# Last output product of a two-layer block: residual, statistics and norm kept in the product's PSUM banks, and the high parts of its rows rounded by ScalarE

## The chip, the cores and the metric

The kernel runs on one core of one Trainium2 chip. The metric is the device time of one execution in microseconds; the median of three runs is used. A core has five engines that run side by side, each with its own queue of instructions taken in order: TensorE (PE in the rows; PEld is its load of stationary weights), VectorE (DVE), ScalarE (ACT), GpSimd (POOL) and SyncE (SP), which here only issues transfers. A trailing q (SPq, ACTq) marks the engine's sequencer, which issues transfers and waits on semaphores. SBUF is the on-chip working memory of 128 partitions, PSUM the memory into which TensorE writes its products: eight banks, each 128 partitions by 512 fp32 values. GpSimd has no access to PSUM in this kernel.

## The reference

Two layers over 1024 latent rows of width 1024 and a context of 256 rows. The first layer (pooling mixer and spatial gating) matters here only as the place of the first output product and its norm. The second layer mixes the rows by a Fourier mixer and by attention with eight heads, gates both, and ends with the step that the change is about:

```python
y = concatenate([yc, yd], axis=-1) @ w_out            # (1024 x 1024) @ (1024 x 1024)
r = ALPHA * x + gate * y                              # x: output of the first layer, gate: one row
mu, var = mean(r), mean((r - mu) ** 2)                # over the 1024 columns of a row
out = (r - mu) * rsqrt(var + EPS) * g + b
```

## The kernel before

Every matmul operand is fp32, cut into a high part (rounded to the fp32r type that TensorE takes) and a low part (the value less its high part); a product is three matmuls, high by high, high by low and low by high. `split` (L102 to L107) makes the two parts: a cast to the high part on VectorE ("v") or ScalarE ("s"), and a subtraction for the low part on VectorE or GpSimd ("p").

**The last product** works on eight row tiles t of 128 rows. `z_split` (L1330) makes yz, the stationary operand of a tile: it cuts the tile's columns of fg (Fourier half) and dg (attention half) into high and low parts, each 128x512; both casts run on VectorE, the low part of fg on VectorE, that of dg on GpSimd. Tiles 0 and 1 are cut near the end of the attention (`block_end`), tile t+2 in the round of tile t; there are two buffers. The weights of the product are four blocks z0 to z3 (wH_z, wL_z and wz in the rows), two for each half of the output columns, loaded through three shared raw buffers; z2 and z3 are cut after the attention, z2 by ScalarE and VectorE, z3 by ScalarE and GpSimd (L143 issues the loads).

The output of a tile is two halves of 512 columns, each summed in one PSUM bank over 24 matmuls (`y_mm`, at L442, of 48 per tile). The first halves of tiles 0 and 1 are made in the last part of the attention; from then on TensorE goes through tile 0 second half, tile 1 second half, tile 2, and so on. Tile 7 is done in four quarters of 256 columns. In this stretch the products take their banks from the four of tag mm; three more of tag tr are free. `z_row` (L1433 to L1437) loads a row tile of the first layer's normalised rows and applies that layer's g and b on GpSimd, two instructions of 128x1024; two buffers xf, tile t+2 again in the round of tile t.

For each half, `z_residual` does three VectorE passes: L1445 multiplies the bank by the gate into r in SBUF, L1446 adds ALPHA times xf, L1447 takes the statistics. Then per tile: L1466 joins the statistics, `rsqrt` (L216) takes a square root on ScalarE and does one Newton step in four instructions of 128x1 on VectorE (L227 to L230), L1477 subtracts the mean and multiplies by g, and L1481 multiplies by the reciprocal root and adds b. L1482 sends the first half from the SyncE queue, the second from ScalarE's. In tile 7, the second half's mean and g are done by ScalarE (L1474) and GpSimd (L1475) instead.

`rsqrt` with n of 1 is also used for the ten tiles of the first layer's norm. The attention's instructions are in an order written out by hand (letters that call pieces, and `pin` that keeps the program's order); the instructions of the last product's norm are not pinned: the framework orders each engine's queue when it builds the program, by the program's order and its own estimates, and puts in the semaphores.

Of the kernel before, what the change touches and what calls it, by code (L numbers as in the profile page):

```python
# [11 lines left out]
AF = mybir.ActivationFunctionType  # L12
ALU = mybir.AluOpType
# [4 lines left out]
P = 128  # L18
D = 1024
# [7 lines left out]
ALPHA = 4 ** 0.25  # L27
# [12 lines left out]
def _f(ap):  # L40
    return ap.bitcast(F32)


def hybrid_block(tc, A):
    nc = tc.nc
    ctx = ExitStack()
    with ctx:
        _body(nc, tc, A, ctx)


def _body(nc, tc, A, ctx):
    def pool(name, bufs=1, side=None, space=None, stack=ctx):
        kw = {}
        if side:
            kw["side"] = side
        if space is not None:
            kw["space"] = space
        return stack.enter_context(tc.tile_pool(name=name, bufs=bufs, reuse_waits="tile", **kw))
# [21 lines left out]
    def ps_mm(name, shape=(P, 512)):  # L80
        return psums[-1].tile(list(shape), F32, tag="mm", name=name, bufs=MM[len(psums)])
# [5 lines left out]
    keep = pool("keep")  # L87
# [15 lines left out]
    def split(dH, dL, src, h="v", l="p", ordered=False):  # L103

        keep = pin if ordered else (lambda ins: ins)
        keep(nc.vector.tensor_copy(dH, src) if h == "v" else nc.scalar.copy(dH, src))  # L106
        keep((nc.gpsimd if l == "p" else nc.vector).tensor_sub(dL, src, _f(dH)))  # L107
# [108 lines left out]
    def rsqrt(sp, v, n, name, bias=EPS, keep=lambda ins: ins):  # L216

        s = sp.tile([P, n], F32, tag="rs_s", name="rs_s" + name, bufs=2)
        e = sp.tile([P, n], F32, tag="rs_e", name="rs_e" + name, bufs=2)
        r = sp.tile([P, n], F32, tag="rs_r", name="rs_r" + name, bufs=2)  # L220
        t = sp.tile([P, n], F32, tag="rs_t", name="rs_t" + name, bufs=2)
        keep(nc.vector.tensor_scalar(e, v, 1.0, bias, op0=ALU.mult, op1=ALU.add))
        nc.scalar.activation(s, e, AF.Sqrt)
        keep(nc.vector.reciprocal(r, s))
        if n == 1:
            u = sp.tile([P, 2], F32, tag="rs_u", name="rs_u" + name, bufs=2)
            keep(nc.vector.scalar_tensor_tensor(t, r, e, r, op0=ALU.mult, op1=ALU.mult))  # L227
            keep(nc.vector.tensor_scalar(u[:, 0:1], r, -0.5, None, op0=ALU.mult))
            keep(nc.vector.tensor_scalar(u[:, 1:2], r, 1.5, None, op0=ALU.mult))
            keep(nc.vector.scalar_tensor_tensor(r, t, u[:, 0:1], u[:, 1:2], op0=ALU.mult, op1=ALU.add))  # L230
            return r
        keep(nc.vector.tensor_mul(t, r, r))
        keep(nc.vector.tensor_mul(t, t, e))
        keep(nc.vector.tensor_scalar(t, t, -0.5, 1.5, op0=ALU.mult, op1=ALU.add))
        keep(nc.vector.tensor_mul(r, r, t))
        return r
# [431 lines left out]
    def v_norm(t, vr):  # L668

        mv = sv.tile([P, 4, 2], F32, tag="mv", name="mv", bufs=2)  # L670
        for j in range(4):
            bs = sv.tile([P, 6], F32, tag="bs", name="bs", bufs=4)
            pin(nc.vector.bn_stats(bs, vr[:, j * P:(j + 1) * P]))
            pin(nc.vector.bn_aggr(mv[:, j, :], bs))
        rs = rsqrt(sv, mv[:, :, 1], 4, "v", keep=pin)
        vH = sv.tile([P, 512], F32R, tag="vH", name="vH", bufs=3)
        vL = sv.tile([P, 512], F32R, tag="vL", name="vL", bufs=3)
        for j in range(4):
            c = slice(j * P, (j + 1) * P)
            pin(nc.vector.tensor_scalar(vr[:, c], vr[:, c], mv[:, j, 0:1], rs[:, j:j + 1],  # L680
                                     op0=ALU.subtract, op1=ALU.mult))
        split(vH, vL, vr, "s", "v", True)
        for i in range(2):
            defer(10.5 + 2.6 * i, lambda i=i: v_gate(i, t, vH[:, i * 256:(i + 1) * 256], vL[:, i * 256:(i + 1) * 256]))
# [83 lines left out]
    def y_mm(ps, yhl, n, c=slice(0, 512)):  # L768

        half_mm(ps, lambda a, k: yhl[:, a, k, :], [x[:, :, c] for x in wo[n]], n % 2)  # L770
# [7 lines left out]
    def row_norm(sp, r, bs, name):  # L778
        mv = sp.tile([P, 2], F32, tag="mv", name="mv" + name, bufs=2)
        nc.vector.bn_aggr(mv, bs.rearrange("p a b -> p (a b)"))  # L780
        rs = rsqrt(sp, mv[:, 1:2], 1, name)
        nb = sp.tile([P, 1], F32, tag="nb", name="nb" + name, bufs=2)
        nc.vector.tensor_scalar(nb, mv[:, 0:1], rs, -1.0, op0=ALU.mult, op1=ALU.mult)
        return rs, nb
# [22 lines left out]
    for t in range(NT):  # L807
        src = A["x"][t * P:(t + 1) * P, :] if t < NL else A["ctx"][(t - NL) * P:(t - NL + 1) * P, :]
# [10 lines left out]
        xt = wp.tile([P, D], F32, tag="raw", name=f"xr{t}", bufs=3)  # L819
        nc.sync.dma_start(out=xt, in_=src)  # L820
        r = S567[t // 4][:, (t % 4) * D:(t % 4 + 1) * D]
        bs = lp.tile([P, 2, 6], F32, tag="bs", name=f"bs{t}", bufs=2)
# [55 lines left out]
    for t in range(NT):  # L878
        lat = t < NL
        c0 = 0 if lat else 256  # L880
        ps = ps_mm("ps_c")
# [147 lines left out]
    mid, rows, yb = {}, {}, None  # L1029
# [114 lines left out]
    for ot, q in units[3:]:  # L1144
        ps = ps_mm("ps_y")
# [184 lines left out]
    def z_split(t, sp):  # L1330
        s = slice(t * P, (t + 1) * P)
        yhl = sp.tile([P, 2, KT, P], F32R, tag="yhl", name=f"yz{t}", bufs=2)
        for i, src in enumerate((fg, dg)):
            k = slice(4 * i, 4 * i + 4)
            split(yhl[:, 0, k], yhl[:, 1, k], src[:, :, s], "v", "p" if i else "v")
        return yhl

    NB = HEADS * 4
# [4 lines left out]
    def block_end(B):  # L1343

        if B == NB - 3:
            st_k.close()
            tail["stack"] = ExitStack()
            fin0 = pool("fin0", stack=tail["stack"])
            tail["y"] = [z_split(t, fin0) for t in range(2)]
        clock[0] += 8.0  # L1350
        tick()
# [74 lines left out]
    gate1 = fin.tile([P, D], F32, name="gate1")  # L1426
    nc.sync.dma_start(out=gate1, in_=gate1_d.partition_broadcast(P))
    vec = {}
# [4 lines left out]
    def z_row(t):  # L1433
        xt = fin.tile([P, D], F32, tag="xt", name=f"xf{t}", bufs=2)
        nc.sync.dma_start(out=xt, in_=xn_d[t * P:(t + 1) * P, :])
        nc.gpsimd.tensor_mul(xt, xt, vec["ab_ln_g"])
        nc.gpsimd.tensor_add(xt, xt, vec["ab_ln_b"])  # L1437
        return xt
# [2 lines left out]
        wo.append(W.use(f"z{n}", ahead=False))  # L1441
    xr = {0: z_row(0), 1: z_row(1)}

    def z_residual(r, bs, ps, c, xt, i):
        nc.vector.tensor_mul(r[:, c], ps, gate1[:, c])  # L1445
        nc.vector.scalar_tensor_tensor(r[:, c], xt[:, c], ALPHA, r[:, c], op0=ALU.mult, op1=ALU.add)  # L1446
        nc.vector.bn_stats(bs[:, i, :], r[:, c])  # L1447

    for t in range(NL):
        last = t == NL - 1  # L1450
        parts = 4 if last else 2
        wd = D // parts
        r = fin.tile([P, D], F32, tag="r", name=f"rz{t}", bufs=2)
        bs = fin.tile([P, 4, 6], F32, tag="bs", name=f"bz{t}", bufs=2)
        for q in range(parts):
            ps = ps_of.get((t, q))
            if ps is None:
                ps = ps_mm("ps_z")
                for n in range(2):
                    y_mm(ps[:, :wd], yz[t], 2 * (q * wd // 512) + n, slice(q * wd % 512, q * wd % 512 + wd))  # L1460
            z_residual(r, bs, ps[:, :wd], slice(q * wd, (q + 1) * wd), xr[t], q)
        if t + 2 < NL:
            yz[t + 2] = z_split(t + 2, fin)
            xr[t + 2] = z_row(t + 2)
        mv = fin.tile([P, 2], F32, tag="mvz", name="mvz", bufs=2)
        nc.vector.bn_aggr(mv, bs[:, :parts].rearrange("p a b -> p (a b)"))  # L1466
        if last:
            nm = fin.tile([P, 1], F32, name="nm")
            nc.vector.tensor_scalar(nm, mv[:, 0:1], -1.0, None, op0=ALU.mult)
        rs = rsqrt(fin, mv[:, 1:2], 1, f"z{t}")  # L1470
        for q in range(2):
            c = slice(q * 512, (q + 1) * 512)
            if last and q:
                nc.scalar.activation(r[:, c], r[:, c], AF.Identity, bias=nm, scale=1.0)  # L1474
                nc.gpsimd.tensor_mul(r[:, c], r[:, c], vec["cd_ln_g"][:, c])  # L1475
            else:
                nc.vector.scalar_tensor_tensor(r[:, c], r[:, c], mv[:, 0:1], vec["cd_ln_g"][:, c],  # L1477
                                               op0=ALU.subtract, op1=ALU.mult)
        for q in range(2):
            c = slice(q * 512, (q + 1) * 512)  # L1480
            nc.vector.scalar_tensor_tensor(r[:, c], r[:, c], rs, vec["cd_ln_b"][:, c], op0=ALU.mult, op1=ALU.add)  # L1481
            (nc.scalar if q else nc.sync).dma_start(out=A["out"][t * P:(t + 1) * P, c], in_=r[:, c])  # L1482
    st_f.close()
    st_ps[0].close()

# [81 lines left out]
```

## Time and profile before

| what | value |
|---|---|
| median of three runs | 1137.46 us (1137.27 to 1138.54) |
| the profiled execution | 1138.53 us |
| its span, first to last instruction | 1136.7 us |
| TensorE busy, mean granted clock | 1077.7 us (95%), 0.977 of full speed |
| VectorE busy | 827.1 us (73%) |
| ScalarE busy | 456.3 us (40%) |
| GpSimd busy | 524.2 us (46%) |

Times in a profile are microseconds from the start of the span. A timeline row gives start, duration, engine, line, operation, output and inputs with their shape, a count of merged instructions, and in brackets how long the engine stood idle before it and what ended that. A duration can hold the time in which an instruction stands in its engine before it can go on. The busy share of a whole kernel is a mean over stages with different limits; the last 100 us are one such stage.

### The profile page before, as it was taken

How to read it: one execution, taken by the hardware profiler on the slowest of the kernel's cores; microseconds unless marked ns; L12 is line 12 of the kernel's file. 1: busy time of each engine (PE TensorE's matmuls, PEld its weight loads, DVE VectorE, ACT ScalarE, POOL GpSimd, SP SyncE). 2: the span in 40 equal slices, each digit the busy share in tenths (PEclk: the TensorE clock that was granted, in tenths of full speed). 3: DMA queues.
4: the chain of work that ended last, by engine and by line, in shares of the span. 5: the costliest groups of instructions: out<-in, count | busy, mean ns of one | idle time of the engine just before them, and what ended most of it. 6: DMA issues, size and time to landing. Idle time of an engine off the chain costs nothing.

```text
span 1136.7 us, 16517 instructions
## 1 busy us (share of the span) xinstructions
PE 1077.7 (95%) x5986; PEld 917.5 (81%) x5986; DVE 827.1 (73%) x1713; ACT 456.3 (40%) x1096; POOL 524.2 (46%) x449
## 2 busy tenths in 40 slices
PE   6999999899999999999999999999999999999884
PEld 4788887778878888897888877889899898887664
DVE  4683547899987767767200175988999989977998
ACT  3421222221211233531021244887888888860000
POOL 2362321555563433112481234855556556657442
PEclk7999999989999999999999999999999999999897
DMA  9630110235543322404311110000000010214221
GB/s 345 222 95 29 47 56 1 60 108 168 166 156 122 104 101 71 148 1 154 106 56 37 34 53 22 1 1 2 1 1 1 1 57 1 75 38 143 85 77 67
DMA packets 46993, 85.58 MB, mean 75 GB/s; under 512 B 2928, under 2 KB 27632, under 8 KB 46912
## 3 DMA queue, kind: packets, MB, share of 16 engines
q1 hardware_dynamic: 44096, 76.60, 21.2%
q0 software_dynamic: 1664, 5.84, 1.4%
q10 hardware_dynamic: 1152, 2.10, 0.5%
q8 instruction: 47, 0.77, 0.3%
q14 instruction: 34, 0.28, 0.1%
HBM read 76.13 MB, written 8.39 MB: 74 GB/s over the span
## 4 chain that ended last, share of the span: by engine, by line
PE 65%; DVE 23%; issue 4%; POOL 3%; ACT 3%; DMA 1%; SPq 0%; DVEq 0%; POOLq 0%; ACTq 0%
PE ps_mm L210 19%; PE ps_o L442 10%; PE s L1096 8%; PE ps_n L442 6%; PE av L1314 5%; PE pt_p L1289 5%; PE acc L363 2%; PE ps_y L1049 2%; DVE acc L499 2%; DVE mx L1255 2%; DVE rz L1477 2%; PE ps_c L210 2%; DVE rz L1446 1%; PE pq L1106 1%; DVE rs_tz L227 1%
## 5 line engine op out<-in xcount | busy, mean ns | idle before, releaser
L1096 PE MATMUL s<-kT,qT 96*128 96x512 f32 (+1 forms) x576 | 147.8, 370 | 3.7 <-ACT p L1267 2.7
L1267 ACT ACTIVATE p<-s,mx 128x512 f32<-128x512 f32 (+1 forms) x192 | 118.7, 624 | 17.1 <-DVE mx L1278 16.1
L1255 DVE TENSOR_REDUCE mx<-s 128x1 f32<-128x512 f32 (+1 forms) x192 | 112.1, 594 | 8.9 <-PE s L1096 7.0
L1298 DVE TENSOR_TENSOR pT<-pt_p,pT 128x512 fp32r<-128x512 f32 x160 | 108.1, 684 | 10.1 <-ACT pT L1294 8.1
L1275 POOL TENSOR_SCALAR p<-p,mx 128x1280 f32<-128x1280 f32 x64 | 85.6, 1341 | 42.1 <-ACT pT L1294 11.9
L1096 PEld LDWEIGHTS s<-kT,qT 96*128 96x128 f32 x576 | 90.7, 189 | 16.3 <-ACT p L1267 6.3
L1294 ACT CAST pT<-pt_p 128x512 fp32r<-128x512 f32 x160 | 92.8, 587 | 19.6 <-PE pt_p L1289 12.3
L1289 PE MATMUL pt_p<-ident,p 128*128 128x128 f32 x640 | 92.9, 273 | 0.9 <-DVE kT L1202 0.5
L1314 PE MATMUL av<-pT,V 128*128 128x256 f32 x480 | 78.9, 291 | 2.1 <-DVE pT L1298 2.1
L1289 PEld LDWEIGHTS pt_p<-ident,p 128*128 128x128 f32 x640 | 74.4, 140 | 7.4 <-ACT q L1112 1.1
L1314 PEld LDWEIGHTS av<-pT,V 128*128 128x128 f32 x480 | 67.5, 189 | 6.8 <-DVE pT L1298 2.5
L442 PE MATMUL ps_o<-wo,yhl 128*128 128x512 f32 x240 | 57.2, 391 | 0.0
L442 PE MATMUL ps_o<-wH_o,yhl 128*128 128x512 f32 x160 | 53.8, 397 | 0.0
L210 PE MATMUL ps_mm<-h,wH_u 128*128 128x512 f32 (+1 forms) x192 | 53.4, 367 | 0.0
L442 PE MATMUL ps_n<-wH_v,h 128*128 128x512 f32 x160 | 52.1, 395 | 0.0
L442 PEld LDWEIGHTS ps_o<-wo,yhl 128*128 128x128 f32 x240 | 44.8, 188 | 9.1
L442 PE MATMUL ps_z<-wz,yz 128*128 128x512 f32 (+1 forms) x216 | 47.3, 376 | 4.8 <-POOL wz L107 2.4
L210 PE MATMUL ps_mm<-h,wH_gb 128*128 128x512 f32 (+1 forms) x192 | 51.7, 357 | 0.0
L210 PE MATMUL ps_mm<-h,wH_ga 128*128 128x512 f32 (+1 forms) x192 | 51.2, 354 | 0.0
L442 PEld LDWEIGHTS ps_z<-wz,yz 128*128 128x128 f32 x216 | 38.2, 193 | 13.0 <-POOL wz L107 2.9
L442 PE MATMUL ps_z<-wH_z,yz 128*128 128x512 f32 (+1 forms) x112 | 36.8, 408 | 8.2 <-DVE yz L106 7.4
L210 PE MATMUL ps_c<-wH_c,h 128*128 128x416 f32 (+1 forms) x160 | 42.3, 341 | 0.0
(390 smaller groups left out, 2876.2 us busy)
## 6 DMA issues: line engine op xcount, KB each, us to landing
rawmm<-in_cd_w_mod SPq DMA_DIRECT2D x16, 512.0 KB, 3.6
wm<-in_ab_w_mod SPq DMA_DIRECT2D x6, 1024.0 KB, 8.2
S<-in_xT SPq DMA_DIRECT2D x8, 640.0 KB, 7.6
rawmg<-in_ab_w_mod SPq DMA_DIRECT2D x8, 512.0 KB, 3.6
raw_o<-in_ab_w_out SPq DMA_DIRECT2D x8, 512.0 KB, 3.8
xr<-in_x SPq DMA_DIRECT2D x8, 512.0 KB, 3.5
xn_d<-S POOLq DMA_DIRECT2D x8, 512.0 KB, 3.0
rawmg<-in_cd_w_mod SPq DMA_DIRECT2D x8, 512.0 KB, 4.3
```

Source lines behind the costliest of these rows:

```text
L210: nc.tensor.matmul(out, lhsT=a, rhs=b, start=(i == 0), stop=(i == n - 1))
L363: pin(nc.tensor.matmul(o, lhsT=a1[w][:, k, c], rhs=tok(h0, K0, x, k, a0, nt), start=(k + n == 0 and j == js[0]), stop=(k == KT - 1 and n = ...
L442: nc.tensor.matmul(ps, lhsT=lhsT(a, kk), rhs=w[b][:, k, :], start=(kk + i == 0), stop=(kk == KT - 1 and i == 2))
L499: pin(nc.vector.scalar_tensor_tensor(o, raw[:, c], s, o, op0=ALU.mult, op1=ALU.add))
L1096: pin(nc.tensor.matmul(out, lhsT=a, rhs=b, start=(i == 0), stop=(i == 2)))
L1255: pin(nc.vector.tensor_reduce(out=mx[:, j:j + 1], in_=ps, axis=AX.X, op=ALU.max))
L1267: pin(nc.scalar.activation(p32[:, e0:e0 + en], sc[e], AF.Exp, bias=mx[:, 3:4], scale=1.0, accum_out=mx[:, 4 + e:5 + e]))
L1275: pin(nc.gpsimd.tensor_scalar(p32, p32, mx[:, 8:9], 1.0, op0=ALU.mult, op1=ALU.mult))
L1289: pin(nc.tensor.transpose(pt[:, kk * 256 + i * P:kk * 256 + (i + 1) * P], P_of[2 * B + i][:, k * P:(k + 1) * P], ident))
L1294: pin(nc.scalar.copy(pT_of[B, kp][:, 0, :], pt))
L1298: pin(nc.vector.tensor_sub(pT[:, 1, :], pt, _f(pT[:, 0, :])))
L1314: pin(nc.tensor.matmul(av, lhsT=vv, rhs=pT[:, hl, kk * 256:(kk + 1) * 256], start=(k == 0 and hl == 0), stop=(k == NT - 1 and hl == 1)))
```

## The change

In the last product, `z_residual` works in place in the product's bank: gate, residual and statistics read the bank, and the first two write it. L1477 works in place in the bank too, and L1481 reads the bank and writes r in SBUF, from where it is sent. Odd parts of a tile take their bank from tag tr, even ones from tag mm. In tile 7 the mean, g and b are applied in quarters (two by VectorE, two by ScalarE and GpSimd, of which ScalarE reads the bank and writes r); its two transfers stay halves. `z_split` makes all casts on ScalarE and all subtractions on GpSimd. In `rsqrt` with n of 1, two instructions on 128x1 change from scalar_tensor_tensor (two tensors and a scalar) to tensor_scalar (one tensor and two scalars per partition).

```diff
--- before.py
+++ after.py
@@ -224,10 +224,10 @@
         keep(nc.vector.reciprocal(r, s))
         if n == 1:
             u = sp.tile([P, 2], F32, tag="rs_u", name="rs_u" + name, bufs=2)
-            keep(nc.vector.scalar_tensor_tensor(t, r, e, r, op0=ALU.mult, op1=ALU.mult))
+            keep(nc.vector.tensor_scalar(t, r, e, r, op0=ALU.mult, op1=ALU.mult))
             keep(nc.vector.tensor_scalar(u[:, 0:1], r, -0.5, None, op0=ALU.mult))
             keep(nc.vector.tensor_scalar(u[:, 1:2], r, 1.5, None, op0=ALU.mult))
-            keep(nc.vector.scalar_tensor_tensor(r, t, u[:, 0:1], u[:, 1:2], op0=ALU.mult, op1=ALU.add))
+            keep(nc.vector.tensor_scalar(r, t, u[:, 0:1], u[:, 1:2], op0=ALU.mult, op1=ALU.add))
             return r
         keep(nc.vector.tensor_mul(t, r, r))
         keep(nc.vector.tensor_mul(t, t, e))
@@ -1332,7 +1332,7 @@
         yhl = sp.tile([P, 2, KT, P], F32R, tag="yhl", name=f"yz{t}", bufs=2)
         for i, src in enumerate((fg, dg)):
             k = slice(4 * i, 4 * i + 4)
-            split(yhl[:, 0, k], yhl[:, 1, k], src[:, :, s], "v", "p" if i else "v")
+            split(yhl[:, 0, k], yhl[:, 1, k], src[:, :, s], "s", "p")
         return yhl
 
     NB = HEADS * 4
@@ -1441,10 +1441,11 @@
         wo.append(W.use(f"z{n}", ahead=False))
     xr = {0: z_row(0), 1: z_row(1)}
 
-    def z_residual(r, bs, ps, c, xt, i):
-        nc.vector.tensor_mul(r[:, c], ps, gate1[:, c])
-        nc.vector.scalar_tensor_tensor(r[:, c], xt[:, c], ALPHA, r[:, c], op0=ALU.mult, op1=ALU.add)
-        nc.vector.bn_stats(bs[:, i, :], r[:, c])
+    def z_residual(bs, ps, c, xt, i):
+
+        nc.vector.tensor_mul(ps, ps, gate1[:, c])
+        nc.vector.scalar_tensor_tensor(ps, xt[:, c], ALPHA, ps, op0=ALU.mult, op1=ALU.add)
+        nc.vector.bn_stats(bs[:, i, :], ps)
 
     for t in range(NL):
         last = t == NL - 1
@@ -1452,13 +1453,15 @@
         wd = D // parts
         r = fin.tile([P, D], F32, tag="r", name=f"rz{t}", bufs=2)
         bs = fin.tile([P, 4, 6], F32, tag="bs", name=f"bz{t}", bufs=2)
+        pss = []
         for q in range(parts):
             ps = ps_of.get((t, q))
             if ps is None:
-                ps = ps_mm("ps_z")
+                ps = (ps_tr if q % 2 else ps_mm)("ps_z")
                 for n in range(2):
                     y_mm(ps[:, :wd], yz[t], 2 * (q * wd // 512) + n, slice(q * wd % 512, q * wd % 512 + wd))
-            z_residual(r, bs, ps[:, :wd], slice(q * wd, (q + 1) * wd), xr[t], q)
+            pss.append(ps[:, :wd])
+            z_residual(bs, pss[q], slice(q * wd, (q + 1) * wd), xr[t], q)
         if t + 2 < NL:
             yz[t + 2] = z_split(t + 2, fin)
             xr[t + 2] = z_row(t + 2)
@@ -1468,18 +1471,22 @@
             nm = fin.tile([P, 1], F32, name="nm")
             nc.vector.tensor_scalar(nm, mv[:, 0:1], -1.0, None, op0=ALU.mult)
         rs = rsqrt(fin, mv[:, 1:2], 1, f"z{t}")
-        for q in range(2):
-            c = slice(q * 512, (q + 1) * 512)
-            if last and q:
-                nc.scalar.activation(r[:, c], r[:, c], AF.Identity, bias=nm, scale=1.0)
+        rows = []
+        for q, ps in enumerate(pss):
+            c = slice(q * wd, (q + 1) * wd)
+            if last and q > 1:
+                nc.scalar.activation(r[:, c], ps, AF.Identity, bias=nm, scale=1.0)
                 nc.gpsimd.tensor_mul(r[:, c], r[:, c], vec["cd_ln_g"][:, c])
+                rows.append(r[:, c])
             else:
-                nc.vector.scalar_tensor_tensor(r[:, c], r[:, c], mv[:, 0:1], vec["cd_ln_g"][:, c],
-                                               op0=ALU.subtract, op1=ALU.mult)
-        for q in range(2):
-            c = slice(q * 512, (q + 1) * 512)
-            nc.vector.scalar_tensor_tensor(r[:, c], r[:, c], rs, vec["cd_ln_b"][:, c], op0=ALU.mult, op1=ALU.add)
-            (nc.scalar if q else nc.sync).dma_start(out=A["out"][t * P:(t + 1) * P, c], in_=r[:, c])
+                nc.vector.scalar_tensor_tensor(ps, ps, mv[:, 0:1], vec["cd_ln_g"][:, c], op0=ALU.subtract, op1=ALU.mult)
+                rows.append(ps)
+        for q, row in enumerate(rows):
+            c = slice(q * wd, (q + 1) * wd)
+            nc.vector.scalar_tensor_tensor(r[:, c], row, rs, vec["cd_ln_b"][:, c], op0=ALU.mult, op1=ALU.add)
+            if parts == 2 or q % 2:
+                c = slice(q * 512 // (parts // 2) - (256 if parts == 4 else 0), (q + 1) * wd)
+                (nc.scalar if c.stop == D else nc.sync).dma_start(out=A["out"][t * P:(t + 1) * P, c], in_=r[:, c])
     st_f.close()
     st_ps[0].close()
 
```

## Rows read from the trace of the kernel before

**Rows 1.** The page's chain that ended last, shares of the span by engine.
```profile
PE 65%; DVE 23%; issue 4%; POOL 3%; ACT 3%; DMA 1%; SPq 0%; DVEq 0%; POOLq 0%; ACTq 0%
```
**Rows 2.** Stretch table: us, busy of PE, PEld, DVE, ACT, POOL, clock, DMA, GB/s.
```profile
360.00:475.00 115.00, 115.00 (x553) 96.83 (x552) 80.95 (x177) 38.13 (x66) 37.31 (x25) 1.00 0.32 104
...
980.00:1000.00 20.00, 20.00 (x143) 18.40 (x142) 18.33 (x46) 17.65 (x48) 11.65 (x11) 1.00 0.18 54
...
1039.00:1061.00 22.00, 22.00 (x98) 17.87 (x96) 21.89 (x31) 0.41 (x2) 13.36 (x6) 1.00 0.21 72
1061.00:1072.00 11.00, 6.79 (x17) 4.95 (x17) 10.97 (x16) 0.20 (x1) 6.08 (x3) 0.69 0.27 96
...
1091.60:1105.70 14.10, 11.54 (x48) 8.86 (x48) 13.85 (x21) 0.20 (x1) 6.49 (x3) 1.00 0.21 74
1105.70:1123.40 17.70, 14.92 (x96) 14.22 (x96) 17.31 (x31) 0.41 (x2) 6.41 (x3) 0.81 0.17 60
```
**Rows 3.** Timeline: VectorE and GpSimd side by side, 1031 to 1034 and 1093 to 1101.
```profile
1031.87 2.37 POOL L1436 TENSOR_TENSOR xf<-xf,v_ab_ln_g 128x1024 f32<-128x1024 f32 x1 [1.05 <-DMA xf<-xn_d]
...
1033.40 0.69 DVE L1445 TENSOR_TENSOR rz<-ps_z,gate 128x512 f32<-128x512 f32 x1 [5.45 <-PE ps_z L442]
...
1093.84 1.31 POOL L107 TENSOR_TENSOR yz<-dg,yz 128x512 fp32r<-128x512 f32 x1 [6.80 <-DVE mvz L1466]
1093.85 0.15 DVE L222 TENSOR_SCALAR rs_ez<-mvz 128x1 f32<-128x1 f32 x1
...
1095.51 2.45 POOL L1436 TENSOR_TENSOR xf<-xf,v_ab_ln_g 128x1024 f32<-128x1024 f32 x1 [0.37 <-DMA xf<-xn_d]
...
1095.69 2.82 DVE L1477 SCALAR_TENSOR_TENSOR rz<-rz,mvz,v_cd_ln_g 128x512 f32<-128x512 f32 x1
...
1098.04 2.73 POOL L1437 TENSOR_TENSOR xf<-xf,v_ab_ln_b 128x1024 f32<-128x1024 f32 x1
1098.43 2.36 DVE L227 SCALAR_TENSOR_TENSOR rs_tz<-rs_rz,rs_ez 128x1 f32<-128x1 f32 x1
```
**Rows 4.** Groups by form, busy us and mean ns; a transfer: KB, us to landing.
```profile
L1477 DVE SCALAR_TENSOR_TENSOR rz<-rz,mvz,v_cd_ln_g 128x512 f32<-128x512 f32 x15 | 23.1, 1554 | 0.0
...
L1445 DVE TENSOR_TENSOR rz<-ps_z,gate 128x512 f32<-128x512 f32 x14 | 9.4, 678 | 5.5 <-PE ps_z L442 5.4
...
L775 DVE SCALAR_TENSOR_TENSOR S<-xr,S 128x512 f32<-128x512 f32 x20 | 13.8, 689 | 0.3
...
L106 ACT CAST wH_z<-raw_z 128x512 fp32r<-128x512 f32 x8 | 5.0, 628 | 0.0
...
xf<-xn_d SPq DMA_DIRECT2D x8, 512.0 KB, 3.4
```
**Rows 5.** Timeline: TensorE where it had waited, tiles 4 and 7.
```profile
1065.42 0.80 PE L442 MATMUL ps_z<-wH_z,yz 128*128 128x512 f32 x1 [4.21 <-DVE yz L106]
...
1117.46 5.92 PE L442 MATMUL ps_z<-wz,yz 128*128 128x256 f32 x48 [2.33 <-DVE rz L1445]
```
**Rows 6.** Timeline: start of the stretch, last two weight blocks and second halves.
```profile
1017.40 2.95 ACT L106 CAST wz<-raw_z 128x1024 fp32r<-128x1024 f32 x3
...
1019.70 5.66 DVE L107 TENSOR_TENSOR wz<-raw_z,wz 128x1024 fp32r<-128x1024 f32 x2
...
1022.06 0.38 SPq L143 DMA_DIRECT2D raw_z<-in_cd_w_out  x1
...
1023.59 4.85 PE L442 MATMUL ps_z<-wz,yz 128*128 128x512 f32 x19
...
1028.48 2.34 POOL L107 TENSOR_TENSOR wz<-raw_z,wz 128x1024 fp32r<-128x1024 f32 x1
...
1030.87 8.36 PE L442 MATMUL ps_z<-wz,yz 128*128 128x512 f32 x29 [2.43 <-POOL wz L107]
```
**Rows 7.** Timeline: VectorE behind the last matmul.
```profile
1127.99 0.41 DVE L1445 TENSOR_TENSOR rz<-ps_z,gate 128x256 f32<-128x256 f32 x1
...
1130.88 1.03 DVE L227 SCALAR_TENSOR_TENSOR rs_tz<-rs_rz,rs_ez 128x1 f32<-128x1 f32 x1
```

## Prediction

> **What bounds the kernel now.** I read the chain that ended last first: TensorE holds 65% of it and VectorE 23% [rows 1]. Then the stretch table, to see where VectorE takes over. Through the first output product (360 to 475 us) TensorE is busy 115.00 of 115.00 us, and 20.00 of 20.00 near the end of the attention; from 1039 to 1061 it still runs without a gap, 22.00 us for two row tiles, so **11.0 us per tile** of 48 matmuls [rows 2]. [...] The timeline says why VectorE is slow. L1477 starts at 1095.69 and takes 2.82 us, ending as GpSimd's L1436 ends (1097.96); L227, on 128x1, starts at 1098.43 and takes 2.36 us, ending when GpSimd's L1437 ends (1100.77) [rows 3]. The same kinds of instruction take 0.69 us at 128x512 in the first layer [rows 4]. So a VectorE instruction that reads two tensors from SBUF stands still while GpSimd's two-tensor instruction runs. One that reads a product in PSUM and one SBUF tensor does not: L1445 at 1033.40 takes 0.69 us in the middle of GpSimd's L1436; nor does a one-tensor instruction on 128x1: L222 at 1093.85 takes 0.15 us beside GpSimd's 1.31 us subtraction [rows 3].
>
> **The change, term by term.**
>
> Waits removed. L1446 and L1477 get the product's bank as one operand, L227 and L230 become one-tensor instructions; L1481 of tiles 0 to 6 reads the bank too. The mean of L1477 is 1554 ns where the free price is 689 [rows 4]; in the round shown, its two runs and L227 alone stood about (1.69-0.65)+(2.82-0.65)+(2.36-0.15), some 5.4 us. The 1.69 and 0.65 are pitches of the chain; the two rows shown carry 2.2 each [rows 3].
>
> Casts moved. Per tile two casts (0.33 us pitch each) and one subtraction (0.6) leave VectorE. ScalarE gains two casts of 0.62 us, by the cast of the same size of the z weights [rows 4]; GpSimd gains one subtraction of 1.31 us [rows 3]. ScalarE had one 0.2 us square root per tile there, so it goes to some 1.5 us per tile. GpSimd goes to 2.45+2.73+2x1.31 = 7.8 us per tile [rows 3], under TensorE's 11.0. The casts also leave VectorE's queue, where the next tile's weights (a TensorE load waited 4.21 us for them at 1065.42 [rows 5]) stood behind the previous tile's norm.
>
> VectorE's new round. Ten 512-wide passes at 0.69 (6.9) and seven small ones at 0.15 to 0.2 (1.1), with some 0.5 for the square root between them: 8.5 us, under 11.0. No row shows a VectorE write to PSUM. Below, nothing less than 0.68 is likely, the price of reading PSUM and writing SBUF (L1445 [rows 4]); above, I take twice that, read and write by turns, for the six passes per tile that write a bank: +4.1, a round of 12.6 us. I take 0.69, as L1445 is the nearest row; the upper end stays for the range. [...]
>
> Banks. A bank is now held until L1481 of its tile, about 8.5 us after the tile's second product. Odd halves rotate through three banks, even ones through four, so TensorE returns to one after three tiles, 33 us. No wait; the wait of 2.33 us for L1445 at 1117.46 [rows 5], with all halves on four banks and VectorE late, goes as well.
>
> With VectorE, GpSimd and ScalarE all under 11.0, **TensorE sets the pace** from tile 2 to the end. Late next would be the low part of yz on GpSimd: ready 1.3 (casts) plus 2.6 us after a tile's last matmul, wanted 11.0 after it.
>
> Start of this stretch. TensorE begins the second half of tile 0 at 1023.59 and stops after 19 matmuls for the low part of the last weight block, which GpSimd starts only at 1028.48; the 29 that are left take 8.36 us instead of 6.6, so tile 2 starts at 1039.1 [rows 6]. That block's load was issued at 1022.06, when VectorE's first wz subtraction gave its buffer back; the two ran from 1019.70, behind tile 2's casts [rows 6]. With the casts on ScalarE behind the wz casts (from 1017.40 [rows 6]), that subtraction can start some 1 to 2 us earlier, and the load with it. But GpSimd has two more 1.3 us subtractions to fit in. Ends: no wait, tile 2 at 1023.6+11.0 = 1034.6; or all four subtractions ahead of the block, as late as now or 3 us later, 1039 to 1042. I take one of tile 3's two ahead of it, a wait of 1.2 us with part of the clock lost, **1036.6**.
>
> Tiles 2 to 7. Five tiles at 11.0 [rows 2] make 55.0; tile 7 in quarters twice 5.8 (48 matmuls in 5.92 at full clock [rows 5]), 11.6. The last matmul ends at 1036.6+66.6 = 1103.2 (now 1123.4).
>
> After the last matmul. The last quarter's L1445 starts at 1127.99, and from there to the end at 1136.7 are 8.7 us; now VectorE comes to it 4.6 us late [rows 7], then at once. L227 there waits for L1475, 1.03 us [rows 7], and becomes 0.15: -0.9. Two 256-wide ScalarE passes instead of one 512-wide ahead of the square root and four final passes instead of two: +0.3 together (bounds 0 and 0.8, their extra fixed parts); the two output transfers of the tile keep their size. So 8.2 us: the span is 1103.2+8.2 = **1111.4**, 25.3 less.
> [...]
>
> At nothing: L227 and L230 in the first layer (ten tiles), hidden under 115.00 us of full TensorE [rows 2]; without that cover they would give 0.5 us each back. The casts of tiles 0 and 1, now on ScalarE amid the attention with the exponentials queued behind: hidden while TensorE is full there [rows 2]; without it, 4x0.62 = 2.5 us. Order of the output transfers: the SyncE and ScalarE queues carry the same ones, and tile t+2's row load (3.4 us [rows 4]) waits on L1446 as before.
>
> The profiled execution took 1138.53 us, 1.8 outside its span and 1.07 above the median of three; the change is subtracted from the median: 1137.46-25.3 = 1112.
>
> **Rivals.**
>
> GpSimd's order is late (chance 0.08). If the row's L1436 and L1437 go ahead of the subtractions, tile t+2's weights come at 1.5+3.4+5.2+2.6 = 12.7 us after tile t, 1.7 late, and TensorE falls to its lower clock for some 2.3 us more, as after 1065 [rows 2, 5]. Every second tile waits, three times 4 us: about 1124. For it: GpSimd's queue is the fullest after TensorE's. Against: the subtractions are ready 3.6 us earlier.
>
> Passes that write PSUM cost double (0.07): a VectorE round of 12.6 against 11.0, 1.6 for three or four tiles that aren't absorbed by slack, no more than 5 with the last tile: 1117 to 1119.
>
> One SBUF operand is enough to wait for GpSimd (0.05), so the change does not do what it says: the round is 14.1 less the 1.26 that moved, eight times, 10 us: 1127. Against it stands L1445 at 1033.40 [rows 3].
>
> TensorE and VectorE take turns in PSUM (0.03), the one that ends slower. Place: every tile from 2 on, when VectorE spends ten passes of 0.69 in banks. Price: up to 6.9 us per tile, 17.9 instead of 11.0; six tiles add 41 to 1112, 1153. It decides from 4.2 us per tile (25.3 over six). Against it: in the first layer VectorE takes every product out of its bank while TensorE is full [rows 2].
>
> **How the numbers follow.** The forecast has 0.77, with its own ends at 1109 (no wait at the start, and 1 us better at the end or in the attention makes 1107) and 1117 (start 3 us later than now). The range 1106 to 1121 takes in the double price and leaves out the late GpSimd, the standing wait and the turns, 0.16. A measurement of this kernel can tell 0.2%, 2.3 us, from no change. All cases but the last are faster by more than that; 0.02 for a late GpSimd that eats everything; 0.03 slower.
>
> **What would show it.** Right: L1477 and L1446 near 0.7 us and L227 near 0.15 everywhere; TensorE busy all of 11.0 us per tile from tile 2 on at a granted clock of 1.00; under 9 us between the last matmul and the end. Wrong: TensorE waiting for yz from GpSimd (first rival), passes on a bank near 1.3 us (second), still 2 to 3 us beside L1436 (third), or a matmul pitch above 0.23 us at full clock (fourth). If tile 2 starts at 1034.6 or 1039 the start term was mis-sized.

## The result and the profile after

| times in us; starts and ends from the start of the span | before | after |
|---|---|---|
| median of four runs | 1137.38 (1137.27 to 1138.54) | 1111.95 (1110.15 to 1113.57) |
| ratio of the times | | 0.977, 95% interval 0.9758 to 0.9782 |
| profiled execution, its span | 1138.53, 1136.7 | 1110.15, 1108.4 |
| TensorE: second half of tile 0 starts | 1023.59 | 1020.08 |
| TensorE: tile 2 starts | 1039.07 | 1033.78 |
| TensorE: last matmul ends | 1123.4 | 1100.2 |
| last matmul to the end of the span | 13.3 | 8.2 |

The medians lie 25.4 us apart, where 25.3 was forecast. The profiled execution of the changed kernel is the fastest of its four, that of the kernel before lies 1.15 us over its median, so their spans lie further apart, 28.3 us. Of these, 3.5 us were won before the stretch of the last product began, 1.8 between that point and tile 2, 17.9 in tiles 2 to 7 (84.3 us before, 66.4 after), and 5.1 behind the last matmul.

The stretch table of the changed kernel answers to [rows 2]; columns as there.

```profile
360.00:475.00 115.00, 115.00 (x554) 96.91 (x553) 77.34 (x178) 38.92 (x69) 37.02 (x25) 1.00 0.32 105
980.00:1000.00 20.00, 19.77 (x142) 17.98 (x141) 17.34 (x43) 17.87 (x46) 12.48 (x12) 1.00 0.10 32
...
1039.00:1061.00 22.00, 22.00 (x97) 18.03 (x97) 21.38 (x55) 2.89 (x7) 17.23 (x11) 1.00 0.43 144
1061.00:1072.00 11.00, 11.00 (x49) 9.02 (x48) 7.84 (x18) 1.34 (x3) 7.65 (x5) 1.00 0.27 95
1072.00:1083.00 11.00, 11.00 (x50) 9.02 (x49) 7.83 (x18) 1.34 (x3) 7.21 (x5) 1.00 0.28 95
1083.00:1094.00 11.00, 11.00 (x71) 9.98 (x70) 7.91 (x20) 0.20 (x1) 4.76 (x2) 1.00 0.14 50
```

Read the length of a stretch against TensorE's busy time, the number behind it: from 1039 on TensorE is busy in every microsecond, one tile in 11.0 us at full clock, where before it was busy 6.79 of 11.00 around 1061 and 11.54 of 14.10 in a round. VectorE (7.84 of 11.00 from 1061 on) now has slack; while it works off a backlog of first rows (21.38 of 22.00 between 1039 and 1061) TensorE does not wait for it, as there are banks enough. GpSimd has 7.2 to 7.7 of 11.0.

The groups by form in the same kernel, 1020 us to the end, answer to [rows 4] (line numbers moved by one to five: L1446 to L1448 are the residual and its statistics, L1482 was L1477, L1486 was L1481).

```profile
L1436 POOL TENSOR_TENSOR xf<-xf,v_ab_ln_g 128x1024 f32<-128x1024 f32 x8 | 19.3, 2411 | 7.7 <-DMA xf<-xn_d 7.7
...
L1482 DVE SCALAR_TENSOR_TENSOR ps_z<-ps_z,mvz,v_cd_ln_g 128x512 f32<-128x512 f32 x14 | 10.2, 747 | 0.0
L1486 DVE SCALAR_TENSOR_TENSOR rz<-ps_z,rs_rz,v_cd_ln_b 128x512 f32<-128x512 f32 x14 | 9.8, 744 | 0.1
...
L1447 DVE SCALAR_TENSOR_TENSOR ps_z<-xf,ps_z 128x512 f32<-128x512 f32 x14 | 9.6, 692 | 5.5 <-POOL xf L1437 5.0
L1446 DVE TENSOR_TENSOR ps_z<-ps_z,gate 128x512 f32<-128x512 f32 x13 | 9.0, 692 | 18.4 <-PE ps_z L442 16.3 <-PE ps_z L1390 2.2
...
L107 POOL TENSOR_TENSOR yz<-fg,yz 128x512 fp32r<-128x512 f32 x6 | 7.8, 1308 | 3.8 <-ACT yz L106 3.8
...
L106 ACT CAST yz<-fg 128x512 fp32r<-128x512 f32 x4 | 2.5, 620 | 21.9 <-PE ps_z L442 21.9
...
L227 DVE TENSOR_SCALAR rs_tz<-rs_rz,rs_ez 128x1 f32<-128x1 f32 x8 | 2.1, 267 | 0.0
```

The mean of the norm's first pass went from 1554 to 747 ns though GpSimd's pair runs as often, and what ends VectorE's idle time is now mostly TensorE (L1446, 16.3 us): the roles of the two have changed. GpSimd gained a little too: L1436 took 2.55 us in the mean before and takes 2.41 now; no run shows why.

The timeline of the changed kernel at the start of the stretch answers to [rows 6].

```profile
1016.27 0.38 SPq L143 DMA_DIRECT2D raw_z<-in_cd_w_out  x1
...
1020.08 4.47 PE L442 MATMUL ps_z<-wz,yz 128*128 128x512 f32 x19
...
1023.41 1.29 POOL L107 TENSOR_TENSOR yz<-dg,yz 128x512 fp32r<-128x512 f32 x1
1024.67 2.33 POOL L107 TENSOR_TENSOR wz<-raw_z,wz 128x1024 fp32r<-128x1024 f32 x1
...
1027.06 6.88 PE L442 MATMUL ps_z<-wz,yz 128*128 128x512 f32 x29 [2.51 <-POOL wz L107]
```

TensorE still stops after 19 matmuls, 2.51 us where it was 2.43. The load of the block was issued 5.8 us earlier, 3.5 of these with TensorE itself, which came to this stretch so much sooner, but GpSimd came to the block only after all four subtractions of tiles 2 and 3, of which the row at 1023.41 is the last; before, two had stood ahead of it.

### The profile page after: what moved, and what is told of

Its sections match the earlier page's. It is cut to its first block, busy times and chain, and to the rows that moved or that the text cites. A ratio compares the mean times of both kernels' runs of the same rounds, so it can differ in the third digit from the quotient of the medians.

```text
span 1108.4 us, 16531 instructions
## 1 busy us (share of the span) xinstructions
PE 1068.5 (96%) x5986; PEld 911.8 (82%) x5986; DVE 770.4 (70%) x1692; ACT 464.6 (42%) x1113; POOL 529.7 (48%) x458
## 4 chain that ended last, share of the span: by engine, by line
PE 76%; DVE 12%; ACT 4%; issue 3%; POOL 3%; DMA 2%; SPq 0%; DVEq 0%; POOLq 0%; ACTq 0%
PE ps_mm L210 22%; PE ps_o L442 10%; PE s L1096 8%; PE ps_z L442 7%; PE ps_n L442 6%; PE av L1314 5%; PE pt_p L1289 5%; PE ps_y L1049 2%; PE acc L363 2%; PE ps_c L210 2%; PE pq L1106 2%; DVE mx L1255 1%; PE po L210 1%; PE pv L1096 1%; DVE kT L1202 1%
## 5 line engine op out<-in xcount | busy, mean ns | idle before, releaser
L698 POOL TENSOR_TENSOR S<-S,bsb 128x256 f32<-128x256 f32 x20 | 16.9, 872 | 51.0 <-DVE S L697 51.0
```

## The experiments

All were timed beside runs of the kernel before on the same chip (medians 1138.26 us in the first four experiments, 1138.25 in the last four).

**Only the casts.** The kernel before with one line changed:

```diff
-            split(yhl[:, 0, k], yhl[:, 1, k], src[:, :, s], "v", "p" if i else "v")
+            split(yhl[:, 0, k], yhl[:, 1, k], src[:, :, s], "s", "p")
```

> The kernel before with one edit: all casts of z_split on ScalarE, all its subtractions on GpSimd. My theory (VectorE's waits for GpSimd set the round, the casts are a small part): a round of VectorE falls from 14.1 us by the 1.26 us that leave it, to about 12.8, still over TensorE's 11.0, and the attention's last part ends about 3 us earlier; together some 10 us less, 1127. L1477 and L227 still stand 2 to 3 us beside GpSimd. Rival (TensorE waited for yz behind VectorE's queue, so that moving the casts is the whole change): all 25 us, 1112.

Measured: 1127.39 us, ratio 0.9902 (0.9885 to 0.9918). 10.9 us went, as my theory had it and not the rival. The groups by form, 1020 to 1130 us, show where VectorE now stood:

```profile
L1481 DVE SCALAR_TENSOR_TENSOR rz<-rz,rs_rz,v_cd_ln_b 128x512 f32<-128x512 f32 x16 | 23.6, 1516 | 0.2
L1446 DVE SCALAR_TENSOR_TENSOR rz<-xf,rz 128x512 f32<-128x512 f32 x14 | 22.9, 1647 | 3.1 <-POOL xf L1437 2.6
L1477 DVE SCALAR_TENSOR_TENSOR rz<-rz,mvz,v_cd_ln_g 128x512 f32<-128x512 f32 x15 | 13.0, 878 | 0.0
```

L1477 and L227 became cheap (878 and 586 ns in the mean) and I had expected them not to; the long times moved to L1446 and L1481 (1647 and 1516 ns). Which instructions are long differs between the two traces; that some are does not. That L1446 and L1481 now fall beside GpSimd's work is my reading; no run shows it by itself. VectorE was busy 74.56 of the 76.00 us from 1034 to 1110, TensorE 69.09. Not all of the gain lies in the rounds: tile 2 starts at 1034.17, 4.9 us sooner than before, of which 1.5 lie in the 29 matmuls behind the wait for the last block (6.87 us instead of 8.36; while they ran in the kernel before, the granted clock was 0.50 from 1031 to 1034 and 1.00 from 1035).

**Only the banks.** Residual, statistics and norm in the banks, seven banks, quarters in the last tile; rsqrt and z_split as before. It is the changed kernel with these lines back:

```diff
-            keep(nc.vector.tensor_scalar(t, r, e, r, op0=ALU.mult, op1=ALU.mult))
+            keep(nc.vector.scalar_tensor_tensor(t, r, e, r, op0=ALU.mult, op1=ALU.mult))
...
-            keep(nc.vector.tensor_scalar(r, t, u[:, 0:1], u[:, 1:2], op0=ALU.mult, op1=ALU.add))
+            keep(nc.vector.scalar_tensor_tensor(r, t, u[:, 0:1], u[:, 1:2], op0=ALU.mult, op1=ALU.add))
...
-            split(yhl[:, 0, k], yhl[:, 1, k], src[:, :, s], "s", "p")
+            split(yhl[:, 0, k], yhl[:, 1, k], src[:, :, s], "v", "p" if i else "v")
```

> The kernel before with the in-place work in the banks (residual, statistics, norm, seven banks, quarters in the last tile), but with rsqrt and z_split as before. My theory: VectorE's round is 8.5 plus 1.3 for casts and subtraction plus up to 2.3 of waiting in L227, 10 to 12 us, near TensorE's 11.0, so most of the gain is here: 15 to 20 us less, 1118 to 1122. Rival (the banks are worth little without the casts on ScalarE): under 8 us, above 1130.

Measured: 1117.99 us, ratio 0.9818 (0.98 to 0.9835): 20.3 of the 26 us, at the upper edge of what was expected; its runs lie wide apart, from 1115.57 to 1119.74 us. One row of the stretch table, and one of the timeline behind the last matmul, which ends at 1106.7:

```profile
1041.00:1106.00 65.00, 65.00 (x330) 55.26 (x329) 62.41 (x126) 1.43 (x7) 36.28 (x17) 1.00 0.28 97
```

```profile
1108.99 0.41 DVE L1446 TENSOR_TENSOR ps_z<-ps_z,gate 128x256 f32<-128x256 f32 x1
```

TensorE is full with VectorE at 62.41 of 65.00, a round of some 10.5 us. So the casts on VectorE cost TensorE nothing here: it never waited for yz. The price of the near tie shows at the end, and the waits of L227 and L230 (585 and 1394 ns in the mean) have a part in it. VectorE comes to the last quarter 2.3 us late, and the span ends 10.8 us after the last matmul, not 8.2.

**Without GpSimd's row instructions.** The kernel before, less these two lines:

```diff
-        nc.gpsimd.tensor_mul(xt, xt, vec["ab_ln_g"])
-        nc.gpsimd.tensor_add(xt, xt, vec["ab_ln_b"])
```

> The kernel before without GpSimd's two instructions per row tile (L1436 and L1437: the first layer's g and b are not applied to the residual rows, so this part of the computation is left out). My theory (VectorE's instructions with two SBUF tensors stand still for those two GpSimd instructions): L1446 and L1477 fall to 0.7 us and L227 to 0.25 without any edit to them, VectorE's round to 9 or 10 us, and about 20 us go, 1117. Rival (these instructions are slow by themselves, or something else holds them): L1477 stays near 1.55 and L227 near 1.65 us in the mean, and under 8 us go.

Measured: 1115.64 us, ratio 0.9799 (0.9784 to 0.9813), 22.6 us less. Two groups of VectorE by form in the kernel before, 1020 to 1137 us:

```profile
L1446 DVE SCALAR_TENSOR_TENSOR rz<-xf,rz 128x512 f32<-128x512 f32 x14 | 15.4, 1111 | 3.0 <-POOL xf L1437 2.6
...
L227 DVE SCALAR_TENSOR_TENSOR rs_tz<-rs_rz,rs_ez 128x1 f32<-128x1 f32 x8 | 13.2, 1655 | 0.1
```

The same in this kernel, 1020 to 1130 us; two lines less in the code, so L1475 is L1477 and L1444 is L1446:

```profile
L1475 DVE SCALAR_TENSOR_TENSOR rz<-rz,mvz,v_cd_ln_g 128x512 f32<-128x512 f32 x15 | 15.1, 1022 | 0.0
...
L1444 DVE SCALAR_TENSOR_TENSOR rz<-xf,rz 128x512 f32<-128x512 f32 x14 | 9.5, 687 | 0.2
...
L227 DVE SCALAR_TENSOR_TENSOR rs_tz<-rs_rz,rs_ez 128x1 f32<-128x1 f32 x8 | 2.5, 313 | 0.1
```

With no edit to VectorE's instructions, L1446 falls from 1111 to 687 ns in the mean and L227 from 1655 to 313. What is left in L1475 (1022 ns, where 0.7 us had been expected) fits GpSimd's one subtraction per tile, which was kept: in the kernel before L1477 takes 1.78 us where it starts with that subtraction (1079.79 and 1093.92) and 0.73 to 0.74 where GpSimd stands idle (1121.33 and 1122.07). This shows the cause of the waits by taking it away; the change avoids it from the other side. An instruction of 128x1 was among those that waited: L227 took 2.36 us in [rows 3], ending with GpSimd's L1437, against 0.31 in the mean here.

**rsqrt back.** The changed kernel with the first four lines of the diff above.

> The changed kernel with L227 and L230 as scalar_tensor_tensor again. My theory: L227 waits up to 2.3 us beside GpSimd in some tiles, but VectorE's round stays under 11.0, so nothing is lost before the last tile, and there at most 1 us: 1111 to 1113. Rival (VectorE's round is so near TensorE's that any wait shows): 2 us in each of six tiles, 1122 to 1124.

Measured: 1111.58 us, ratio 0.9765 (0.975 to 0.9779), no different from the change itself. The groups by form of this kernel:

```profile
L230 DVE SCALAR_TENSOR_TENSOR rs_rz<-rs_tz,rs_uz 128x1 f32<-128x1 f32 x8 | 5.6, 704 | 0.1
L227 DVE SCALAR_TENSOR_TENSOR rs_tz<-rs_rz,rs_ez 128x1 f32<-128x1 f32 x8 | 4.1, 506 | 0.0
```

The waits are there (506 and 704 ns in the mean, 267 without) and hidden in VectorE's slack. In the last tile, where nothing hides them, the two took 0.38 and 0.52 us, 0.36 together more than the tensor_scalar pair: GpSimd's work there is cut into quarters of 0.7 us, so there is less to stand for. The rsqrt edit is worth nothing that can be measured beside the other two; with the banks and the casts on VectorE it was not tried by itself.

**The change once more**, as a control:

> The changed kernel itself once more, as a control beside the next three on the same chip: 1110 to 1114. If the spread of its runs comes from TensorE's clock behind its wait for the last weight block, a slower execution shows its 29 matmuls after that wait at 8.4 us instead of 6.9, and the rest unchanged.

Measured: 1112.00 us (1111.4 to 1112.45), ratio 0.977 (0.9756 to 0.9785); span of the profiled execution 1109.6. Its timeline at the wait for the last weight block:

```profile
1026.93 8.27 PE L442 MATMUL ps_z<-wz,yz 128*128 128x512 f32 x29 [2.48 <-POOL wz L107]
```

The wait is as long as in the first profile (2.48 and 2.51 us), but the 29 matmuls behind it take 8.27 instead of 6.88 us: the granted clock was 0.89 in the mean from 1020 to 1036, and 1.00 in the same stretch of the first. That is 1.4 us, more than the difference of the spans (1.2).

**Tiles 0 and 1 cut as before.** The changed kernel, with

```diff
-            split(yhl[:, 0, k], yhl[:, 1, k], src[:, :, s], "s", "p")
+            split(yhl[:, 0, k], yhl[:, 1, k], src[:, :, s], *(("v", "p" if i else "v") if t < 2 else ("s", "p")))
```

> The changed kernel with the cut of tiles 0 and 1 (four casts and two subtractions amid the attention) on the engines of before. My theory: these six VectorE instructions delay the attention's pieces, TensorE's waits for pT and p of 1.0 to 1.4 us near 967, 973 and 1002 come back, and the second half of tile 0 starts 2.5 to 3 us later: about 1114.5. Rival (the earlier start in the changed kernel is scatter of the attention between executions): no change, 1112.

Measured: 1114.81 us (1114.45 to 1116.1), ratio 0.9797 (0.9783 to 0.9812), 2.8 us over the control on the same chip; the second half of tile 0 starts at 1022.87, in the control at 1019.99. The waits of TensorE between 950 and 1005 us, in the timeline of the kernel before:

```profile
967.09 0.63 PE L1314 MATMUL av<-pT,V 128*128 128x256 f32 x3 [1.10 <-DVE pT L1298]
...
972.70 0.96 PE L1096 MATMUL s<-kT,qT 96*128 96x512 f32 x3 [1.38 <-ACT p L1267]
...
1002.50 1.23 PE L1314 MATMUL av<-pT,V 128*128 128x256 f32 x7 [1.01 <-DVE pT L1298]
```

The same waits are back in this kernel's timeline:

```profile
966.37 0.62 PE L1314 MATMUL av<-pT,V 128*128 128x256 f32 x3 [1.08 <-DVE pT L1298]
...
971.98 0.96 PE L1096 MATMUL s<-kT,qT 96*128 96x512 f32 x3 [1.39 <-ACT p L1267]
...
1001.78 1.22 PE L1314 MATMUL av<-pT,V 128*128 128x256 f32 x7 [1.03 <-DVE pT L1298]
```

The one wait that the timeline of the changed kernel lists there is

```profile
966.94 0.62 PE L1096 MATMUL s<-kT,qT 96*128 96x256 f32 x3 [0.23 <-ACT p L1267]
```

From 950 to 1010 us TensorE was idle for 3.51 us in the kernel before, for 3.52 here and for 0.51 in the changed kernel: the six VectorE instructions of those tiles stood in the way of the attention's own pieces. They were long, as some of them seem to have waited for GpSimd in their turn: the six took 7.3 us in the kernel before, where free ones of their kinds (0.42 us a cast, 0.68 a subtraction) make 3.0. One is a cast, with one SBUF tensor as input, beside a GpSimd subtraction, both from the timeline of the kernel before:

```profile
1000.22 1.28 POOL L107 TENSOR_TENSOR yz<-dg,yz 128x512 fp32r<-128x512 f32 x1 [0.87 <-DVE yz L106]
...
1000.39 1.39 DVE L106 CAST yz<-dg 128x512 fp32r<-128x512 f32 x1
```

The cast ends 0.28 us behind the subtraction. So two SBUF tensors are not what every waiting instruction has. How much of the 2.8 us these waits are, no run shows.

**z3's low parts by VectorE.** The changed kernel, with

```diff
-        W.state[f"z{n}"]["eng"] = (("s", "v"), ("s", "p"))[n - 2]
+        W.state[f"z{n}"]["eng"] = ("s", "v")
```

> The changed kernel with the low parts of the last weight block z3 made by VectorE instead of GpSimd. My theory: TensorE's wait of 2.5 us for it goes, tile 2 starts 2.7 us earlier and the rest follows, 1109. Rival (the time reappears as a wait for the row tiles xf or for yz of tiles 2 and 3 on GpSimd): no change.

Measured: 1107.50 us (1106.03 to 1107.83), ratio 0.9729 (0.9714 to 0.9743), 4.5 us under the control, whose runs on the same chip begin at 1111.4. The second halves of tiles 0 and 1 in its timeline:

```profile
1019.98 11.04 PE L442 MATMUL ps_z<-wz,yz 128*128 128x512 f32 x48
```

All 48 in one piece; tile 2 starts at 1030.9, 4.1 us before the control. The expectation had 2.7 us there, 1.4 too little, as it left out the slow matmuls behind the wait: the 29 in the control take 8.27 us, and here all 48 take 11.04. This is the fastest version of all.

**Four banks.** The changed kernel, with

```diff
-                ps = (ps_tr if q % 2 else ps_mm)("ps_z")
+                ps = ps_mm("ps_z")
```

> The changed kernel with all parts of a tile on the four banks of tag mm. My theory: a bank is held until L1486 of its tile; TensorE wants the bank of tile 0 for tile 2 at 1033.8, but it comes free only about 1043, so it waits some 9 us there, and 2 to 3 us more in the last tile: 1122 to 1125. Rival (the extra banks matter little, as VectorE is quick enough): 1112 to 1114.

Measured: 1121.68 us (1121.26 to 1122.38), ratio 0.9858 (0.9841 to 0.9874), 9.7 us over the control. TensorE's two waits after the start, in its timeline:

```profile
1042.21 0.79 PE L442 MATMUL ps_z<-wH_z,yz 128*128 128x512 f32 x1 [7.28 <-DVE rz L1486]
1105.36 5.92 PE L442 MATMUL ps_z<-wz,yz 128*128 128x256 f32 x48 [0.46 <-DVE rz L1486]
```

Tile 2 waits 7.28 us until tile 0's norm has read its bank, and the first matmuls behind it take longer (0.79 us where 0.39 is usual; tile 2 takes 13.1 us where the next takes 11.0): together some 9 us. In the kernel before, behind the wait at 1065.42, the matmul of 0.80 us [rows 5] came with a granted clock of 0.50 (1066 to 1071). In the last tile the wait is 0.46 us, not 2 to 3. So with four banks the change gives back 9.7 of its 26 us.

## Why the prediction was right

The time came out at the forecast, and most steps hold by themselves. Two terms were wrong, in opposite directions, and cancelled only in part: tile 2 starts 2.8 us ahead of the forecast of 1036.6 in the profiled execution, and 1.6 ahead in the control. That the median is met to 0.1 us is luck in part, as the two profiled executions lie on opposite sides of their medians (1.15 us over it before, 1.8 under it after).

- **Waits removed: right.** L1477 at 689 was forecast and 747 ns measured for L1482; L227 at 0.15, measured 0.27, which is this form's own price and no wait (261 to 273 ns in all eight). The cause is shown by the run without GpSimd's row instructions. One row was read too neatly: L1477 ends at 1098.51, not with L1436 but 0.55 us behind it, as if it had run only once GpSimd was done; only L227 ends with L1437 (1100.79 and 1100.77) [rows 3]. The third rival (one SBUF operand is enough to wait) falls for the instructions that were changed, with L1447, which reads xf beside a bank at 692 ns; for a cast of 128x512 from SBUF to SBUF it holds (1.39 us beside GpSimd, 0.42 free).
- **VectorE's new round: right.** 8.5 us were forecast; with TensorE setting the pace VectorE is busy 7.8 to 7.9 of 11.0. No write to PSUM had been seen; it costs next to nothing: L1446 has 692 ns where it wrote SBUF at 678 [rows 4], L1447 has 692 where the free price was 689. The upper bound, double, and with it the second rival fall.
- **Banks: right**, no wait with seven, and four_banks shows what they are worth, 9.7 us.
- **Tiles 2 to 7: right.** 66.6 us forecast, 66.4 measured, at a granted clock of 1.00. That also refutes the fourth rival (turns in PSUM): VectorE works in banks all the while.
- **GpSimd's order: right.** The subtractions of a tile stand ahead of its row instructions, and TensorE never waits for yz; the first rival did not occur. But the remark that the casts left VectorE's queue, where TensorE's next weights stood, was worth nothing by itself: with the banks alone and the casts on VectorE, TensorE is full.
- **Start of the stretch: the wait was under-sized.** I took 1.2 us and 0.8 of clock, with one subtraction of tile 3 ahead of the block, from ends of none and four; all four stood ahead, and the wait was 2.5 us, with 1.4 us of clock more in the control than in the first profile.
- **Casts of tiles 0 and 1 "at nothing": the term that failed, in its sign.** I bounded it by 0 and a loss of 2.5 us, because TensorE was full from 980 to 1000 [rows 2]. These instructions also run near 967 and 1002, outside that stretch, and the trace of the kernel before has TensorE waiting there (1.10, 1.38 and 1.01 us). Moving them gained 2.8 us. With 0.7 us by which this execution was ahead already at 60 us (59.70 against 60.38), before anything that the change touches, it makes up the early start of 3.5 us, and more than covers the wait above.
- **After the last matmul: right in the sum** (8.2 forecast and measured). L227 went from 1.03 to 0.27 us, 0.76 less where 0.9 was put. Of this the rsqrt edit has the smaller part: rsqrt_back gives it 0.36 for L227 and L230 together, beside L1479 in quarters of 0.7 us, where L1475 took 1.26 in one piece.

What each part is worth depends on what else is in: banks alone 20.3 us, casts alone 10.9, all edits 26.3 in the control. Once TensorE sets the pace, a shorter VectorE round is worth nothing more until the end (with the banks alone TensorE was full, 65.00 of 65.00 us, with VectorE at 62.41). Of the casts the attention's 2.8 us remain and some of the 2.6 us of backlog at the end, which no run divides between the casts and the waits of L227 and L230.

## What to carry to other kernels

When VectorE's small instructions have durations like GpSimd's, lay the two engines side by side in the timeline: here an instruction with two SBUF tensors that ended with GpSimd's (L227, 2.36 us), or 0.55 us behind it (L1477, 2.82 us), was waiting. A PSUM operand freed those of 128x512 (L1477, from 1554 to 747 ns in the mean), and one tensor with scalars those of 128x1 (L227, from 1655 to 267), where taking other work off VectorE left as long times in other instructions (1647 and 1516 ns). One SBUF tensor instead of two is no safe sign by itself: the cast of 128x512 waited (1.39 us, 0.42 free). Keeping work in a product's bank holds the bank longer (with four banks TensorE waited 7.28 us for one), so count the banks from TensorE's side first. Before an edit is called hidden, look at the waits of the full engine over the whole time in which the moved instructions run, not over one stretch of it.

## What was not expected of the hardware

Behind nearly the same wait of TensorE, 2.43 to 2.51 us, the 29 matmuls were quick in two of the nine profiled executions that have it (6.88 us in the first profile of the change, 6.87 with only the casts) and slow in seven (8.22 to 8.49 us, among them the kernel before and the control). The granted clock from 1020 to 1036 was 1.00 in the first profile of the change, and 0.89 in the kernel before and in the control. A good part of the spread of the runs, 1110.15 to 1113.57 us, may be this difference, but only profiled executions show it. An instruction of 128x1 with two scalars per partition (L227, 267 ns) takes longer than the one with immediates beside it (144 ns), and longer than the free scalar_tensor_tensor that it replaced (214 to 220 ns): here the new form won only where the old one waited.
